# Neighbourhood mixer of a transformer trunk: queries two pairs ahead, keys projected apart, part of the output projection held back, values packed as high beside low parts

## Chip, cores and metric

One core of a Trainium2 chip runs the whole program. The metric is device time in microseconds (us) of one execution. PE is the matmul engine, PEld its weight load, DVE the vector engine, ACT the scalar engine, POOL GpSimd, SP the queue that issues most transfers.

## The reference

Four post-norm sublayers in each of two layers: half-step FFN, token mixer, memory attention, half-step FFN, on 512 tokens of width 1024 in float32. The mixer of layer 0 is called AB below. The change lies in the mixer of layer 1, C, for 16 heads of width 64 on an 8 x 64 grid:

```python
q, k, v = jnp.split(h @ w_in, 3, axis=-1)
...
    s = jnp.einsum('bwhd,bawjhd->bhwaj', q_r, k_nb).astype(jnp.float32) * scale
    s = s + bias.astype(jnp.float32)[None]
    p = jax.nn.softmax(s.reshape(B, C_HEADS, GRID_W, kh * kw), axis=-1)
...
    return jnp.einsum('bhwaj,bawjhd->bwhd', p, v_nb)
...
return o @ w_out
```

Each token sees all 8 rows and a window of 16 columns around its own. Then x = LN(alpha*x + mixer(x)).

## The kernel before

Float32 accuracy is reached with split operands: every operand is a high part and a low part (`split`: ACT writes the high part, DVE the difference), and a product is three matmuls (`mm3`: high x high, high x low, low x high).

`mixer_c` works in eight pairs of heads. For a pair, `queries_keys` projects queries and keys (24 matmuls of 512 columns each, two PSUM banks), `weights_of` makes eight score blocks (two matmuls of 192 or 256 columns each, into a bank of tag "a"), adds the bias and takes the minimum on DVE, the exponential on ACT, and normalises (192-column blocks on DVE, 256-column blocks on POOL). `turned` transposes the weights on PE into four banks of tag "t" (two for each head), each drained by one ACT cast and one DVE subtraction. `attend` multiplies by the values into one bank of tag "d". `values` projects the values of four heads (two pairs) at once, into slabs that POOL first clears (`padded`), since the stationary operand of one head has zeros in the other head's columns.

In the loop, step `pair` holds the projections of pair+1 (on odd steps with the values of the next two pairs ahead of them), `turned` of its own weights, the scores of pair+1, and its own `attend`. The output projection is done at step 4 (for the first four pairs), at step 7 (two pairs) and after the loop (the last two, with the layer norm of each 128-token tile, the transposes of the normed tile, and then the memory attention).

All instructions are recorded first and put into an order by `Graph.emit`, a list scheduler with estimated durations; on the chip each engine runs its own list in that order. Banks and slabs are handed out by tag: 27 slabs, two raw weight buffers, 14 `t2` buffers, three banks "a", two "d", three "t". A bank is given out again when the last reader of its former contents is done. Every recorded instruction has line L140 in the profile, so instructions are told apart by their tiles: `a`, `d`, `t` are the banks.

Of the kernel before, what the change touches and what calls it, by code (L numbers as in the profile page):

```python
# [12 lines left out]
F32 = mybir.dt.float32  # L13
F32R = mybir.dt.float32r
# [3 lines left out]
ALU = mybir.AluOpType  # L18
AX = mybir.AxisListType

P = 128
D = 1024
S = 512
NT = S // P
# [225 lines left out]
class Kernel:  # L250
# [94 lines left out]
            )  # L345
        return got

    def w_rows(self, w, r0):

        src = w[r0 : r0 + 256, :].rearrange("(b p) f -> p b f", p=P)  # L350
        return self.weights([(lambda r: r, src)], (2, D), [lambda r, i=i: r[:, i, :] for i in range(2)])

# [53 lines left out]
        nc.vector.scalar_tensor_tensor(out=x, in0=x, scalar=nmu, in1=g, op0=ALU.add, op1=ALU.mult)  # L406
        nc.vector.scalar_tensor_tensor(out=x, in0=x, scalar=r, in1=b, op0=ALU.mult, op1=ALU.add)

    def down_bank(self, acts, wts, t, h, coef):

        ps = self.ps("d")
        for i, (act, w) in enumerate(zip(acts, wts)):
            self.mm3(ps, [z[:, t * P : (t + 1) * P] for z in act], w, i == 0, i == len(acts) - 1)
        v = self.x[t][:, h * 512 : (h + 1) * 512]
        self.nc.vector.scalar_tensor_tensor(out=v, in0=ps, scalar=coef, in1=v, op0=ALU.mult, op1=ALU.add)
# [494 lines left out]
    def mixer_c(self, ln_i, last):  # L910
# [2 lines left out]

        ends = [self.slab(F32R, (P, KB, P)) for _ in range(2)]

        def values(grp):

            wv = self.w_cols_k(w_in, 2 * D + 256 * grp)
            vp = [self.padded() for _ in range(2)]
            if grp == 0:  # L920
                for dst, lo in ((slice(64, 128), 0), (slice(0, 64), 448)):
                    nc.scalar.copy(ends[0][:, :, dst], self.xh[:, :, lo : lo + 64])
                    nc.vector.tensor_copy(ends[1][:, :, dst], self.xl[:, :, lo : lo + 64])
            for t in range(NT):
                ps = self.ps("a")
                for k in range(KB):
                    mv = [z[:, k % 4, :] for z in wv[k // 4]]
                    x = self.xT(k, 64 + t * P, 64 + (t + 1) * P) if t < 3 else [z[:, k, :] for z in ends]
                    self.mm3(ps[:, :256], x, mv, k == 0, k == KB - 1)
                for b in range(2):  # L930
                    dst = []
                    for z in vp[b]:
                        v = z[:, t].rearrange("p v c -> p (v c)")
                        dst.append(bass.AP(v.tensor, v.offset, [list(v.ap[0]), [192, 2], [1, 64]]))
                    self.split(ps[:, b * P : (b + 1) * P].rearrange("p (v c) -> p v c", v=2), *dst)
            return vp

        def queries_keys(w, b, first):


            cuts = [(0, 128), (128, 256), (256, 512)] if first else [(0, 512)]
            ps = self.ps("a")
            for lo, hi in cuts:
                self.project(w[0][b], ps, lo, hi)
            qs = self.pair()
            for s, z in enumerate(qs):
# [5 lines left out]
            ps = self.ps("a")  # L952
            for lo, hi in [(0, 256), (256, 512)] if first else cuts:
                self.project(w[1][b], ps, lo, hi)
            ks = [self.pair() for _ in range(2)]
            for s, (h, l) in enumerate(ks):
# [5 lines left out]
            return list(zip(qs, ks))  # L962

        def biases(pair):

# [15 lines left out]
                got.append(dst)  # L981
            return got

        def weights_of(qk, bias):

            got = []
            for (q, k), table in zip(qk, bias):
# [38 lines left out]

        def attend(pts, vp):
            po = self.ps("d")
            ends_ = bass.AP(po[:].tensor, po[:].offset, [list(po[:].ap[0]), [384, 2], [1, P]])
            for s in range(2):  # L1030
                for j in range(4):
                    dst = po[:, j * P : j * P + 256] if j < 3 else ends_
                    mv = [z[:, (j % 2) * 256 : (j % 2) * 256 + 256] for z in pts[s][j // 2]]
                    if j == 3:
                        mv = [z.rearrange("p (c n) -> p c n", c=2) for z in mv]
                    self.mm3(
                        dst, [z[:, j, s, :] for z in vp], mv, s == 0 and j == 0, s == 1 and j == 3, skip_group_check=True
                    )
            return self.split_t2(po)

        def weights_qk(grp):
            return self.w_cols(w_in, 256 * grp), self.w_cols(w_in, D + 256 * grp)

        vp = values(0)
        wqk = weights_qk(0)
        qk = queries_keys(wqk, 0, True)
        acts, us = [], weights_of(qk, biases(0))
        for pair in range(8):

            now = vp[pair % 2]  # L1050
            if pair % 2 == 1 and pair < 7:
                vp = values(pair // 2 + 1)
                wqk = weights_qk(pair // 2 + 1)
            if pair < 7:
                qk = queries_keys(wqk, (pair + 1) % 2, False)
            if pair == 4:
                self.down(acts[:4], self.w_rows(w_out, 0) + self.w_rows(w_out, 256), 1.0 / ALPHA)
            if pair == 7:
                self.down(acts[4:6], self.w_rows(w_out, 512), 1.0 / ALPHA)
            pts = turned(us)  # L1060
            if pair < 7:
                us = weights_of(qk, biases(pair + 1))
            acts.append(attend(pts, now))
        gb = self.load_ln(ln_i)
        self.down(acts[6:], self.w_rows(w_out, 768), 1.0 / ALPHA, {"gb": gb, "last": last})


    def memory(self, i, ln_i, last):
# [195 lines left out]
```

## Time and profile before

| what | us |
|---|---|
| median of 3 runs (2286.45 to 2290.6) | 2288.22 |
| profiled execution | 2287.07 |
| its span | 2285.3 |

| engine | busy us | share of the span | instructions |
|---|---|---|---|
| PE | 2227.2 | 97% | 11376 |
| DVE | 1414.9 | 62% | 2124 |
| ACT | 873.2 | 38% | 1418 |
| POOL | 298.8 | 13% | 407 |

Busy is an average over stages. What a stage can give is what PE loses in it: idle time, and time at a lower granted clock. The mixer C and the tail that leads into the memory attention lie from about 1468.7 to 1757.4 us of the span.

### The profile page before, as it was taken

Reading aid. Unit: us, or ns where it says so; the run is one execution under the profiler, and the core shown is the slowest. Engines: PE = TensorE matmul, PEld = TensorE weight load, DVE = VectorE, ACT = ScalarE, POOL = GpSimd, SP = SyncE. Lnnn points to the kernel's source line nnn. Section 1 sums busy time; section 2 is a strip of 40 time slices with the busy share of each in tenths; the row PEclk is TensorE's granted clock in tenths of the full one; section 3 lists DMA queues with packets and bytes.
Section 4 is the critical chain, followed back from the end, with each engine's and each line's share of the span. In section 5 each row is a group of like instructions: output and inputs, shape, how many; then the busy total and the mean of one; then the engine's idle time right before and its main releaser. Section 6 shows DMA issues by size and latency. Waiting matters only on the chain.

```text
span 2285.3 us, 28345 instructions
## 1 busy us (share of the span) xinstructions
PE 2227.2 (97%) x11376; PEld 1887.8 (83%) x11376; DVE 1414.9 (62%) x2124; ACT 873.2 (38%) x1418; POOL 298.8 (13%) x407
## 2 busy tenths in 40 slices
PE   8999999999999999999999999989998999999998
PEld 7888888778898888888988888888787988888886
DVE  5666646788745666664666665556667557566653
ACT  4333323476433433333333333344454444333331
POOL 0000203543100100020100012223221001000021
PEclk9999999999999999999999999989999999999999
DMA  6333241003423233324233224121122433312241
GB/s 203 127 118 111 83 146 45 19 20 101 140 93 126 78 111 111 111 83 134 79 111 109 71 78 164 49 65 65 61 79 93 131 128 111 108 63 75 90 145 37
DMA packets 168211, 221.09 MB, mean 97 GB/s; under 512 B 6160, under 2 KB 136848, under 8 KB 168080
## 3 DMA queue, kind: packets, MB, share of 16 engines
q1 hardware_dynamic: 165008, 208.80, 28.1%
q0 software_dynamic: 3072, 10.49, 1.4%
q8 instruction: 89, 1.46, 0.3%
q14 instruction: 42, 0.34, 0.1%
HBM read 217.17 MB, written 4.19 MB: 97 GB/s over the span
## 4 chain that ended last, share of the span: by engine, by line
PE 92%; DVE 4%; ACT 1%; POOL 1%; DMA 1%; issue 1%; SPq 0%; POOLq 0%; ACTq 0%; DVEq 0%
PE a L140 58%; PE d L140 25%; PE t L140 9%; DVE slab L140 2%; DVE x L140 1%; POOL lny L140 1%; ACT junk L140 1%; ACT slab L140 1%; DVE t L140 1%; DMA x<-x 0%; DVE xl L140 0%; DMA raw<-mem_w_kv 0%; ACT t L140 0%; SPq L140 0%; ACT xh L140 0%
## 5 line engine op out<-in xcount | busy, mean ns | idle before, releaser
L140 PE MATMUL a<-xh,slab 128*128 128x512 f32 (+2 forms) x3184 | 962.4, 383 | 0.0
L140 PEld LDWEIGHTS a<-xh,slab 128*128 128x128 f32 x3184 | 592.2, 188 | 116.0 <-DVE mn L140 0.2
L140 PE MATMUL d<-slab,slab 128*128 128x512 f32 (+2 forms) x2592 | 609.8, 384 | 12.6 <-ACT slab L140 8.8
L140 PE MATMUL a<-xl,slab 128*128 128x512 f32 (+2 forms) x1592 | 609.3, 383 | 0.0
L140 PEld LDWEIGHTS d<-slab,slab 128*128 128x128 f32 x2592 | 469.9, 190 | 108.4 <-ACT slab L140 12.6
L140 DVE TENSOR_TENSOR slab<-raw,slab 128x1024 fp32r<-128x1024 f32 x316 | 393.4, 1261 | 75.4 <-ACT slab L140 54.8
L140 ACT CAST slab<-raw 128x1024 fp32r<-128x1024 f32 x316 | 320.4, 1050 | 307.2 <-DMA raw<-ffn_w_gate 141.6
L140 PEld LDWEIGHTS a<-xl,slab 128*128 128x128 f32 x1592 | 299.8, 188 | 57.4
L140 DVE TENSOR_TENSOR slab<-slab,slab 128x1024 fp32r<-128x1024 f32 (+2 forms) x208 | 241.5, 1185 | 19.4 <-ACT slab L140 18.4
L140 ACT CAST slab<-slab 128x1024 fp32r<-128x1024 f32 (+1 forms) x144 | 140.2, 1001 | 238.5 <-DVE slab L140 238.1
L140 DVE TENSOR_TENSOR slab<-a,t 128x512 f32<-128x512 f32 x56 | 38.7, 692 | 270.2 <-PE a L140 270.2
L140 PE MATMUL a<-slab,slab 128*128 128x256 f32 (+2 forms) x1312 | 193.9, 296 | 7.4 <-DVE slab L140 3.7
L140 ACT CAST slab<-t 128x512 fp32r<-128x512 f32 (+1 forms) x213 | 118.2, 580 | 209.5 <-DVE t L140 137.8
L140 DVE SCALAR_TENSOR_TENSOR x<-d,x 128x512 f32<-128x512 f32 x232 | 158.2, 686 | 61.0 <-PE d L140 60.1
L140 PEld LDWEIGHTS a<-slab,slab 128*128 128x128 f32 x1312 | 171.8, 194 | 20.2 <-DVE slab L140 6.7
L140 POOL TENSOR_TENSOR x<-x,slab 128x512 f32<-128x512 f32 x24 | 46.0, 1947 | 782.2 <-DVE x L140 782.2
L140 DVE TENSOR_TENSOR slab<-t,slab 128x512 fp32r<-128x512 f32 (+1 forms) x213 | 134.3, 655 | 20.1 <-ACT slab L140 19.1
L140 ACT ACTIVATE t<-a 128x512 f32<-128x512 f32 (+2 forms) x104 | 57.4, 552 | 227.9 <-PE a L140 205.8
L140 PE MATMUL t<-slab,slab 128*128 128x512 f32 x576 | 143.2, 391 | 0.0
L140 PE MATMUL a<-slab,xh 128*128 128x256 f32 (+1 forms) x576 | 125.4, 313 | 4.2 <-ACT xh L140 4.2
L140 PEld LDWEIGHTS t<-slab,slab 128*128 128x128 f32 x576 | 106.7, 188 | 25.3 <-DVE slab L140 2.4
L140 POOL TENSOR_TENSOR t<-t,l 128x256 f32<-128x256 f32 (+2 forms) x104 | 86.5, 847 | 303.4 <-DVE l L140 303.4
(84 smaller groups left out, 1643.9 us busy)
## 6 DMA issues: line engine op xcount, KB each, us to landing
raw<-ffn_w_gate SPq DMA_DIRECT2D x40, 1024.0 KB
raw<-ffn_w_up SPq DMA_DIRECT2D x40, 1024.0 KB
slab<-ffn_w_down SPq DMA_DIRECT2D x64, 512.0 KB
raw<-ffn_w_down SPq DMA_DIRECT2D x12, 1024.0 KB
raw<-mem_w_kv SPq DMA_DIRECT2D x8, 1024.0 KB
raw<-mem_w_kv SPq DMA_DIRECT2D x16, 512.0 KB
raw<-mem_w_q SPq DMA_DIRECT2D x8, 1024.0 KB
raw<-mem_w_o SPq DMA_DIRECT2D x8, 1024.0 KB
```

The lines of the kernel that those rows point to most:

```text
L140: op.call = lambda: fn(*args, **kw)
```

## The change

- The projections of one pair become two functions. `queries(pair)` uses a bank "d" and is recorded two pairs ahead, between `turned` and the scores; `keys(pair)` uses a bank "t" and stays one pair ahead, at the step's start.
- `values` is called for one 128-token tile at a time: two tiles behind each `attend`, in a bank "t". The slabs hold for each head 64 columns of high parts beside 64 of low parts; nothing is cleared.
- `attend` makes two matmuls a block in place of three: the stationary operand is [high | low], the moving one the weights' high, then low part, so a fourth product (low x low) is in it too. Each head has a bank "d" of its own; the high half (partitions 0 to 63) and the low half (64 to 127) are added by an ACT copy and a DVE addition per head, and the sum is split again by one ACT cast and one DVE subtraction.
- The output projection: the first four pairs' part becomes eight single banks ("a"), `share(0)` to `share(7)`: two after `turned` of step 6, one behind its `attend`, two ahead of `turned` of step 7, three behind it. Their weights come in four 512 KB loads. The last four pairs' part all stands after the loop, in the banks with the layer norm.

```diff
-        def values(grp):
-
-            wv = self.w_cols_k(w_in, 2 * D + 256 * grp)
-            vp = [self.padded() for _ in range(2)]
...
-                        dst.append(bass.AP(v.tensor, v.offset, [list(v.ap[0]), [192, 2], [1, 64]]))
-                    self.split(ps[:, b * P : (b + 1) * P].rearrange("p (v c) -> p v c", v=2), *dst)
-            return vp
...
+        def values(grp, t):
+
+            if t == 0:
+                wv[0] = self.w_cols_k(w_in, 2 * D + 256 * grp)
+                vp[grp] = [self.slab(F32R, (P, 2, 4, 2, 64)) for _ in range(2)]
...
+            ps = self.ps("t" if grp else "a")
+            for k in range(KB):
+                mv = [z[:, k % 4, :] for z in wv[0][k // 4]]
+                x = self.xT(k, 64 + t * P, 64 + (t + 1) * P) if t < 3 else [z[:, k, :] for z in ends]
+                self.mm3(ps[:, :256], x, mv, k == 0, k == KB - 1)
+            z = vp[grp][t // 2][:, t % 2]
+            self.split(ps[:, :256].rearrange("p (v c) -> p v c", v=4), z[:, :, 0], z[:, :, 1])
+
+        def queries(pair, first=False):
+
+            if pair % 2 == 0:
+                wq[0] = self.w_cols(w_in, 128 * pair)
+            ps = self.ps("a" if first else "d")
+            for lo, hi in [(0, 128), (128, 256), (256, 512)] if first else [(0, 512)]:
+                self.project(wq[0][pair % 2], ps, lo, hi)
+            qs[pair] = self.pair()
...
+        def keys(pair, first=False):
+
+            if pair % 2 == 0:
+                wk[0] = self.w_cols(w_in, D + 128 * pair)
+            ps = self.ps("a" if first else "t")
+            for lo, hi in [(0, 256), (256, 512)] if first else [(0, 512)]:
+                self.project(wk[0][pair % 2], ps, lo, hi)
+            ks[pair] = [self.pair() for _ in range(2)]
...
-        def attend(pts, vp):
-            po = self.ps("d")
...
+        def attend(pts, pair):
+            pos = [self.ps("d") for _ in range(2)]
+            for s, po in enumerate(pos):
...
+                    dst = po[:, j * P : j * P + 256] if j < 3 else po.rearrange("p (c n) -> p c n", c=4)[:, 0:4:3]
+                    v = vp[pair // 2][j // 2][:, j % 2, 2 * (pair % 2) + s].rearrange("p z c -> p (z c)")
+                    for i, z in enumerate(pts[s][j // 2]):
+                        mv = z[:, (j % 2) * 256 : (j % 2) * 256 + 256]
+                        mv = mv.rearrange("p (c n) -> p c n", c=2) if j == 3 else mv
+                        nc.tensor.matmul(
+                            dst, v, mv, start=j == 0 and i == 0, stop=j == 3 and i == 1, skip_group_check=True
+                        )
+
+            o = self.t2(F32)
+            for s, po in enumerate(pos):
+                y = o[64 * s : 64 * s + 64]
+                nc.scalar.copy(y, po[64:128])
+                nc.vector.tensor_tensor(out=y, in0=po[0:64], in1=y, op=ALU.add)
...
+        def share(n):
+
+            h, t = divmod(n, 4)
+            if t == 0:
+                wo[h] = [z for r in range(2) for z in self.w_rows(w_out, 256 * r, 512 * h)]
+            self.down_bank(acts[:4], wo[h], t, h, 1.0 / ALPHA, "a")
...
+        for t in range(NT):
+            values(0, t)
+        queries(0, True)
+        keys(0, True)
+        queries(1)
+        us = weights_of(0)
...
             if pair < 7:
-                qk = queries_keys(wqk, (pair + 1) % 2, False)
-            if pair == 4:
-                self.down(acts[:4], self.w_rows(w_out, 0) + self.w_rows(w_out, 256), 1.0 / ALPHA)
-            if pair == 7:
-                self.down(acts[4:6], self.w_rows(w_out, 512), 1.0 / ALPHA)
+                keys(pair + 1)
+            else:
+                for n in range(3, 5):
+                    share(n)
             pts = turned(us)
+            if pair < 6:
+                queries(pair + 2)
+            else:
+                for n in (0, 1) if pair == 6 else (5, 6, 7):
+                    share(n)
             if pair < 7:
-                us = weights_of(qk, biases(pair + 1))
-            acts.append(attend(pts, now))
+                us = weights_of(pair + 1)
+            acts.append(attend(pts, pair))
+            if pair < 6:
+                for t in range(2):
+                    values(pair // 2 + 1, 2 * (pair % 2) + t)
+            elif pair == 6:
+                share(2)
         gb = self.load_ln(ln_i)
-        self.down(acts[6:], self.w_rows(w_out, 768), 1.0 / ALPHA, {"gb": gb, "last": last})
+        self.down(acts[4:], self.w_rows(w_out, 512) + self.w_rows(w_out, 768), 1.0 / ALPHA, {"gb": gb, "last": last})
```

In the order of the instructions this shows at three places. In PE's list, at step 2 (keys of pair 3 and weights of pair 2; `a_2283` and `t_2283` are the bank of the keys before and now, `t_2286` to `t_2292` the four turned banks, `d_2299` the bank of the queries of pair 4), this stood before:

```order
L140 MATMUL a_2283_2364<-xh_2_83,slab_2239_2320 128x512
L140 MATMUL t_2286_2367<-ident_1_78,t2_2257_2338 128x128 x3
...
L140 MATMUL t_2288_2369<-ident_1_78,t2_2258_2339 128x128 x2
...
L140 MATMUL t_2290_2371<-ident_1_78,t2_2268_2349 128x128 x3
...
L140 MATMUL a_2301_2382<-slab_2284_2365,slab_2282_2363 128x192
...
L140 MATMUL d_2320_2401<-slab_2287_2368,slab_2222_2303 128x256
...
L140 MATMUL t_2292_2373<-ident_1_78,t2_2269_2350 128x128 x2
...
L140 MATMUL d_2320_2401<-slab_2287_2368,slab_2222_2303 128x256
```

And this stands now:

```order
L140 MATMUL t_2283_2364<-xh_2_83,slab_2237_2318 128x512
L140 MATMUL t_2286_2367<-ident_1_78,t2_2255_2336 128x128 x3
...
L140 MATMUL t_2288_2369<-ident_1_78,t2_2256_2337 128x128 x2
...
L140 MATMUL d_2299_2380<-xh_2_83,slab_2295_2376 128x512
...
L140 MATMUL t_2290_2371<-ident_1_78,t2_2266_2347 128x128 x3
...
L140 MATMUL t_2292_2373<-ident_1_78,t2_2267_2348 128x128 x2
...
L140 MATMUL d_2299_2380<-xh_2_83,slab_2296_2377 128x512
...
L140 MATMUL a_2308_2389<-slab_2284_2365,slab_2250_2331 128x192 x2
...
L140 MATMUL d_2327_2408<-slab_2287_2368,slab_2229_2310 128x256 x3
```

Before, three turned banks, two half-done score blocks and one value product stand between the last projection and the fourth bank. Now 14 of the 24 query matmuls stand between the second and the third bank, and the other ten between the fourth and the scores.

In DVE's list at the same place (draining the keys' bank and the turned banks), before:

```order
L140 TENSOR_TENSOR slab_2284_2365<-a_2283_2364,slab_2284_2365 64x512 x2
L140 TENSOR_TENSOR slab_2287_2368<-t_2286_2367,slab_2287_2368 128x512
L140 TENSOR_TENSOR slab_2289_2370<-t_2288_2369,slab_2289_2370 128x512
L140 TENSOR_TENSOR slab_2285_2366<-a_2283_2364,slab_2285_2366 64x512 x2
L140 TENSOR_TENSOR slab_2291_2372<-t_2290_2371,slab_2291_2372 128x512
L140 ISA t2_2298_2379,mn_2302_2383<-a_2301_2382,t2_2296_2377 128x192
```

And now, where the keys' bank has tag "t" too, so that `t_2290` waits for its last reader (slab_2285):

```order
L140 TENSOR_TENSOR slab_2284_2365<-t_2283_2364,slab_2284_2365 64x512 x2
L140 TENSOR_TENSOR slab_2287_2368<-t_2286_2367,slab_2287_2368 128x512
L140 TENSOR_TENSOR slab_2289_2370<-t_2288_2369,slab_2289_2370 128x512
L140 TENSOR_TENSOR slab_2285_2366<-t_2283_2364,slab_2285_2366 64x512 x2
L140 TENSOR_TENSOR slab_2291_2372<-t_2290_2371,slab_2291_2372 128x512
L140 TENSOR_TENSOR slab_2293_2374<-t_2292_2373,slab_2293_2374 128x512
L140 TENSOR_TENSOR slab_2342_2423<-raw_2340_2421,slab_2341_2422 128x1024
L140 ISA t2_2305_2386,mn_2309_2390<-a_2308_2389,t2_2303_2384 128x192
...
L140 SCALAR_TENSOR_TENSOR slab_2300_2381<-d_2299_2380,slab_2300_2381 64x512 x2
```

The draining has the same order as before; behind it, a weight split and the first two score blocks now stand ahead of the draining of the queries' bank `d_2299`.

In PE's list in the tail (`d_2597` and up before, `d_2599` and up now: banks of the last output products; x0 to x3: the normed tiles, transposed into `t`), before:

```order
L140 MATMUL d_2597_2678<-slab_2576_2657,slab_2549_2630 128x512
...
L140 MATMUL d_2598_2679<-slab_2576_2657,slab_2549_2630 128x512
...
L140 MATMUL t_2586_2667<-ident_1_78,x0_4_85 128x128 x4
...
L140 MATMUL d_2605_2686<-slab_2576_2657,slab_2549_2630 128x512
...
L140 MATMUL d_2606_2687<-slab_2576_2657,slab_2549_2630 128x512
...
L140 MATMUL t_2594_2675<-ident_1_78,x1_5_86 128x128 x4
...
L140 MATMUL t_2602_2683<-ident_1_78,x2_6_87 128x128 x4
```

And now:

```order
L140 MATMUL d_2599_2680<-slab_2573_2654,slab_2437_2518 128x512
...
L140 MATMUL t_2588_2669<-ident_1_78,x0_4_85 128x128 x4
...
L140 MATMUL d_2600_2681<-slab_2573_2654,slab_2437_2518 128x512
...
L140 MATMUL d_2607_2688<-slab_2573_2654,slab_2437_2518 128x512
...
L140 MATMUL t_2596_2677<-ident_1_78,x1_5_86 128x128 x4
...
L140 MATMUL d_2608_2689<-slab_2573_2654,slab_2437_2518 128x512
...
L140 MATMUL t_2604_2685<-ident_1_78,x2_6_87 128x128 x4
...
L140 MATMUL t_2615_2696<-ident_1_78,raw_2614_2695 128x128 x4
```

Six matmuls a bank (two pairs) have become twelve (four pairs), and the transposes of a tile stand among the products of the tile after next.

## Rows read from the trace of the kernel before

**Rows 1.** The page, part 1 (busy us, share, instructions) and the granted clock by slice

```profile
PE 2227.2 (97%) x11376; PEld 1887.8 (83%) x11376; DVE 1414.9 (62%) x2124; ACT 873.2 (38%) x1418; POOL 298.8 (13%) x407
...
PEclk9999999999999999999999999989999999999999
```

**Rows 2.** Windows over mixer C and its tail: window, length, busy by engine, clock

```profile
1468.70:1498.20 29.50, 28.16 (x233) 27.39 (x232) 15.38 (x26) 9.01 (x20) 5.47 (x6) 1.00 0.24 74
1498.20:1530.50 32.30, 26.29 (x122) 21.83 (x120) 19.51 (x50) 18.44 (x43) 8.27 (x18) 0.79 0.22 72
...
1563.50:1584.50 21.00, 19.30 (x102) 16.59 (x100) 17.09 (x33) 13.50 (x29) 11.78 (x19) 0.92 0.20 63
...
1728.00:1757.40 29.40, 21.31 (x103) 16.70 (x102) 24.83 (x42) 13.14 (x22) 7.26 (x8) 0.88 0.10 32
sum 288.70, PE 263.38 PEld 229.67 DVE 183.91 ACT 131.26 POOL 78.25; mean PE 29.26 PEld 25.52 DVE 20.43 ACT 14.58 POOL 8.69
```

**Rows 3.** Windows over the six stretches of half clock in that stage

```profile
1500.90:1511.10 10.20, 7.96 (x23) 6.35 (x24) 8.09 (x26) 6.99 (x20) 4.74 (x9) 0.50 0.10 32
...
sum 27.20, PE 23.80 PEld 21.84 DVE 22.46 ACT 17.00 POOL 6.59; mean PE 3.97 PEld 3.64 DVE 3.74 ACT 2.83 POOL 1.10
```

**Rows 4.** Timeline at step 0: start, us, engine, what, in brackets idle before

```profile
1520.23 1.17 ACT L140 CAST slab<-a 64x512 fp32r<-64x512 f32 x2 [3.18 <-PE a L140]
...
1523.39 0.39 PE L140 MATMUL d<-slab,slab 128*128 128x256 f32 x1 [1.44 <-ACT slab L140]
...
1523.47 1.29 DVE L140 TENSOR_TENSOR slab<-t,slab 128x512 fp32r<-128x512 f32 x2
...
1524.22 0.66 PE L140 MATMUL t<-ident,t 128*128 128x128 f32 x4 [0.22 <-DVE slab L140]
...
1524.80 1.40 DVE L140 TENSOR_TENSOR slab<-a,slab 64x512 fp32r<-64x512 f32 x2
```

**Rows 5.** Waits from 1498 to 1757: total us, times, longest

```profile
PE d L140 <- ACT slab L140: 7.5, 6, 1.4
PE t L140 <- DVE nmu L140: 4.2, 1, 4.2
```

**Rows 6.** Groups by form, 1478 to 1728: busy us, mean ns, idle before

```profile
L140 DVE TENSOR_TENSOR slab<-raw,slab 128x1024 fp32r<-128x1024 f32 x26 | 34.9, 1361 | 0.1
...
L140 ACT CAST slab<-raw 128x1024 fp32r<-128x1024 f32 x25 | 25.5, 1050 | 0.1
...
L140 DVE TENSOR_TENSOR slab<-a,slab 64x512 fp32r<-64x512 f32 x32 | 22.0, 689 | 32.0 <-PE t L140 21.0 <-ACT slab L140 10.6
L140 DVE TENSOR_TENSOR slab<-t,slab 128x512 fp32r<-128x512 f32 x32 | 21.2, 687 | 0.6 <-ACT slab L140 0.2
...
L140 POOL MEMSET slab<- 128x1024 f32 x10 | 9.3, 954 | 29.5 <-PE d L140 23.3 <-PE a L140 6.2
```

**Rows 7.** The chain in order of time: start, us, what

```profile
559.31 5.91 DMA raw<-mem_w_kv
...
1618.11 11.03 PE a L140 x48
...
1757.37 22.65 PE a L140 x189
```

**Rows 8.** Windows over mixer AB and its tail, columns as in group 2

```profile
240.00:480.00 240.00, 239.35 (x1111) 195.28 (x1110) 155.87 (x279) 91.79 (x165) 72.60 (x81) 1.00 0.22 70
...
555.00:600.00 45.00, 40.69 (x224) 33.45 (x223) 34.55 (x54) 19.18 (x31) 5.28 (x8) 1.00 0.32 101
```

**Rows 9.** Timeline in the tail of mixer C

```profile
1745.80 1.27 DVE L140 SCALAR_TENSOR_TENSOR x<-x,lny,slab 128x1024 f32<-128x1024 f32 x1
...
1747.22 1.94 PE L140 MATMUL t<-ident,x 128*128 128x128 f32 x8 [4.17 <-DVE nmu L140]
```

**Rows 10.** Timeline: normalising on DVE beside POOL, and without

```profile
1531.38 1.23 DVE L140 TENSOR_SCALAR t<-t,l 128x192 f32<-128x192 f32 x2
...
1660.82 0.55 DVE L140 TENSOR_SCALAR t<-t,l 128x192 f32<-128x192 f32 x2
```

More of the change, by code (lines that the diff above doesn't have):

```diff
@@ L346, in w_cols512, with w_rows @@
         return got
-    def w_rows(self, w, r0):
+    def w_rows(self, w, r0, c0=None):
+        if c0 is not None:
+            src = w[r0 : r0 + 256, c0 : c0 + 512].rearrange("(b p) f -> p b f", p=P)
+            hi, lo = self.weights([(lambda r: r, src)], (2, 512), [lambda r: r])[0]
+            return [(hi[:, b], lo[:, b]) for b in range(2)]
         src = w[r0 : r0 + 256, :].rearrange("(b p) f -> p b f", p=P)
@@ L407, in layer_norm, with down_bank @@
         nc.vector.scalar_tensor_tensor(out=x, in0=x, scalar=r, in1=b, op0=ALU.mult, op1=ALU.add)
-    def down_bank(self, acts, wts, t, h, coef):
-        ps = self.ps("d")
+    def down_bank(self, acts, wts, t, h, coef, tag="d"):
+        ps = self.ps(tag)
         for i, (act, w) in enumerate(zip(acts, wts)):
@@ L914, in mixer_c @@
         ends = [self.slab(F32R, (P, KB, P)) for _ in range(2)]
-        def values(grp):
-            wv = self.w_cols_k(w_in, 2 * D + 256 * grp)
-            vp = [self.padded() for _ in range(2)]
[L920 to L933, printed above, removed]
-                        dst.append(bass.AP(v.tensor, v.offset, [list(v.ap[0]), [192, 2], [1, 64]]))
-                    self.split(ps[:, b * P : (b + 1) * P].rearrange("p (v c) -> p v c", v=2), *dst)
-            return vp
@@ L938, in queries_keys @@
[L938 to L946, printed above, removed]
+        def values(grp, t):
+            if t == 0:
+                wv[0] = self.w_cols_k(w_in, 2 * D + 256 * grp)
+                vp[grp] = [self.slab(F32R, (P, 2, 4, 2, 64)) for _ in range(2)]
+                if grp == 0:
+                    for dst, lo in ((slice(64, 128), 0), (slice(0, 64), 448)):
+                        nc.scalar.copy(ends[0][:, :, dst], self.xh[:, :, lo : lo + 64])
+                        nc.vector.tensor_copy(ends[1][:, :, dst], self.xl[:, :, lo : lo + 64])
+            ps = self.ps("t" if grp else "a")
[5 more added lines that the diff above has]
+            self.split(ps[:, :256].rearrange("p (v c) -> p v c", v=4), z[:, :, 0], z[:, :, 1])
@@ L947, in queries_keys @@
+        def queries(pair, first=False):
[5 more added lines that the diff above has]
+            qs[pair] = self.pair()
+            for s, z in enumerate(qs[pair]):
                 own, other = slice(64 * s, 64 * s + 64), slice(64 - 64 * s, 128 - 64 * s)
@@ L951, in queries_keys @@
                 )
[L952 to L956, printed above, removed]
+        def keys(pair, first=False):
[5 more added lines that the diff above has]
+            ks[pair] = [self.pair() for _ in range(2)]
+            for s, (h, l) in enumerate(ks[pair]):
                 own, other = slice(64 * s, 64 * s + 64), slice(64 - 64 * s, 128 - 64 * s)
@@ L961, in queries_keys @@
                     nc.vector.tensor_tensor(out=l[half], in0=ps[own], in1=h[own].bitcast(F32), op=ALU.subtract)
-            return list(zip(qs, ks))
         def biases(pair):
@@ L982, in biases, with weights_of @@
             return got
-        def weights_of(qk, bias):
+        def weights_of(pair):
             got = []
-            for (q, k), table in zip(qk, bias):
+            for q, k, table in zip(qs.pop(pair), ks.pop(pair), biases(pair)):
                 both = [self.t2(F32), self.t2(F32)]
@@ L1025, in turned @@
             return pts
-        def attend(pts, vp):
-            po = self.ps("d")
-            ends_ = bass.AP(po[:].tensor, po[:].offset, [list(po[:].ap[0]), [384, 2], [1, P]])
-            for s in range(2):
+        def attend(pts, pair):
+            pos = [self.ps("d") for _ in range(2)]
+            for s, po in enumerate(pos):
                 for j in range(4):
[L1032 to L1047, printed above, removed]
+                    dst = po[:, j * P : j * P + 256] if j < 3 else po.rearrange("p (c n) -> p c n", c=4)[:, 0:4:3]
[6 more added lines that the diff above has]
+                        )
@@ new lines, in attend @@
+            o = self.t2(F32)
[3 more added lines that the diff above has]
+                nc.vector.tensor_tensor(out=y, in0=po[0:64], in1=y, op=ALU.add)
+            return self.split_pair(o)
+        def share(n):
[3 more added lines that the diff above has]
+            self.down_bank(acts[:4], wo[h], t, h, 1.0 / ALPHA, "a")
@@ L1048, in mixer_c @@
+        vp, qs, ks, acts = {}, {}, {}, []
+        wv, wq, wk, wo = [None], [None], [None], {}
+        for t in range(NT):
[4 more added lines that the diff above has]
+        us = weights_of(0)
         for pair in range(8):
[L1050 to L1053, printed above, removed]
             if pair < 7:
-                qk = queries_keys(wqk, (pair + 1) % 2, False)
```

## The prediction

> **What bounds the kernel now.** I read the page's busy table and clock line first: PE is busy for 97% of the span at nearly full clock, and no other engine comes near it [rows 1]. So the kernel is bound by PE, and a change can win only by taking matmuls out or by filling the places where PE idles or runs at half clock. The clock line shows one dull slice; windows over it show that this is mixer C, the stage that the change rewrites. In the 288.7 us from 1468.7 to 1757.4, PE is busy for 263.4, so it idles for 25.3, and of these 8.1 lie in the tail and 6.0 in the first steps [rows 2]. The granted clock in the stage is below 1 in four windows. Cut into its six low stretches, it stands at 0.50 (1.2 in place of 2.4 GHz) for 27.2 us, in which PE is busy for 23.8; work done at half rate takes twice its time, so this costs 23.8 / 2 = 11.9 us [rows 3]. Together the stage loses 25.3 + 11.9 = 37.2 us.
>
> Where does PE idle? The timeline of step 0 shows the pattern that repeats in most steps: PE has done its transposes and stands for 1.44 us until ACT has cast the first turned bank (which comes behind two of the key copies), and again 0.22 us for the fourth bank [rows 4]. The table of waits counts six such waits, 7.5 us, and one wait of 4.2 us in the tail on the layer norm's chain [rows 5]. Before the stretches of half clock PE had stood in such waits; in the first one it still idles for 2.2 of 10.2 us [rows 3]. No wait of PE or ACT on a weight transfer is in that table.
>
> **The change part by part.**
>
> *Products.* Value products go from 24 to 16 a pair, 64 fewer in all. 189 matmuls of 256 columns in a row took 22.65 us, 0.12 each [rows 7]: 64 x 0.12 = 7.7 us of PE are gone, and they lie on the path, since PE is the bound. All other matmuls stay; the output products are 192 as before, only moved.
>
> *Filler behind the transposes.* 24 query matmuls (512 columns, 11.03 / 48 = 0.23 each [rows 7], 5.5 us) now stand between the turned banks and the first value product. The wait of 1.44 us and its companions are covered by them, and at the start by `queries(1)` and `keys(1)` the waits on the first keys and scores. If all of it is covered and nothing new waits, only what lies outside the steps stays.
>
> *New waits on banks.* The keys' bank now has tag "t", so the third turned bank must wait until it is drained. Count from the end of the keys' projection. ACT works on three key copies, two turned banks and the fourth copy at 1.17 / 2 = 0.58 each; DVE takes two key differences (1.40), then two turned ones (1.29), then two key ones (1.40) [rows 4]. DVE can start at 0.7, is at the turned banks at about 2.5 (ACT is there no earlier) and done with them at 3.9, and frees the bank at about 5.2. PE has eight transposes (about 1.1; four took 0.66 with the last one's drain [rows 4]) and 14 query matmuls (3.2) until then, and asks at 4.3: it stands for about 0.9 to 1.0 us, of which a busy table shows 0.8, since the matmul in flight still drains. Queued behind it on PE are the fourth bank, ten query matmuls and the scores, and so the exponentials of the next pair. Behind that, eight score blocks share three "a" banks, and the second head's value products need the queries' bank, behind a weight split (1.36 us on DVE [rows 6]) in every second step. I take 0.5 a step for these, between 0 (all hidden) and 1.4 (the split's whole length). That is 1.3 us for each of seven steps, 9.1 in all. Where DVE is late at the keys, each 0.7 us of lateness comes on top.
>
> *Engines beside PE.* An attend gains two DVE additions of 64x512 in place of a difference of 512, and one more difference: 2 x 0.69 more for each pair, 11 us. Eight output additions (16 banks in place of 24 outside the tail's own) go, 8 x 0.69 = 5.5 us [rows 6], and the value splits become half as many. DVE is busy for 183.9 of 288.7 us [rows 2]; 189 of 262 would be 72%. It is covered by PE's work on the average, and dear only where it comes in bursts. POOL loses 16 clears of 0.95 us, 15 us [rows 6]; ten lie in these rows. They are worth nothing by themselves, for POOL is busy for 78 of 289 us [rows 2]. SP issues two more loads (four of half the size in place of two), hidden behind the keys and scores of step 6; exposed, they cost what the last rival says. The bias loads and bias work on POOL stay where they were.
>
> One row speaks against more DVE work here. Normalising two 192-column blocks took 1.23 us beside a POOL instruction and 0.55 us without one [rows 10]. The Trainium skill (SBUF — State Buffer, Who interferes with whom) says that DVE instructions with two SBUF inputs, or in a two-port mode, share an exclusive port pair with GpSimd, and that the second to come is fully blocked. The trace agrees for the normalising with the numbers above; for the new difference (both inputs in SBUF) no row of this stage shows it. By the rule it could be held up as the normalising was, an estimate of (1.23 - 0.55) / 2 = 0.34 us a pair on DVE; by its row alone it costs 0.69 and no more.
>
> *Tail.* Before, PE does six matmuls a bank (2.8 us a tile) while DVE needs two additions (1.4), two passes of the norm (2 x 1.27 [rows 9]) and the split of the transposes (as long as two turned banks, 1.29 [rows 4]), some 5.2 us a tile. So PE waits, once for 4.17 us [rows 9], and the clock falls (0.88 [rows 2]); idle is 8.1 us. With twelve a bank PE has 5.5 us a tile and the norm hides beside it. Mixer AB's tail has just this form (twelve a bank, then the memory attention), and idles for 4.3 of 45 us at full clock [rows 8]. I take 4.3.
>
> *Sum.* Left after the change: 1.3 us in the first window (the lead-in, unchanged), 1.0 at the first scores, 9.1 in steps 0 to 6, 0.5 in step 7, 4.3 in the tail, 1.5 for one stretch of half clock, since waits of about 1 us remain: 17.7. Gain: 7.7 + 37.2 - 17.7 = 27.2 us. The profiled execution took 2287.07 (span 2285.3), which makes 2259.9; it lies 1.15 under the median of the runs, so I predict **2261 us**.
>
> Bounds: mixer AB's main part, built in the same way, idles for 0.65 in 240 us [rows 8], and steps that lose only 0.4 each (3.2) leave 9.3 in all with 0.5 at the start and no half clock: gain 35.6, time 2252.6. At the other end a step loses as much as the worst between 1563.5 and 1584.5: 1.7 idle and 21 x 0.08 = 1.7 of clock [rows 2], 3.4 for each of seven steps: 23.8 + 1.3 + 1.0 + 0.5 + 4.3 = 30.9, gain 14.0, time 2274.
>
> **Rivals.**
>
> - *Full cover* (2253): the bank waits hide, because DVE reaches the keys early. For it speaks mixer AB; against it the count above, in which 5.2 stands against 4.3.
> - *DVE late in every step* (2274): the weight splits, the longer attend and the shared port push the keys' draining back, PE waits as long as before and its clock falls again. For it speaks that DVE is already busy for 17.1 of 21.0 us in a step without values [rows 2]; against it that each step now has 48 of the 96 value matmuls of two pairs in it, 5.8 us of PE time.
> - *The cover is worth nothing* (2280.5): every wait returns in another place, and only the 7.7 us of products are won.
> - *Slower* (2294): weights come late. Queries two pairs ahead, keys and values now ask for their loads one by one through two raw buffers. A load that PE must wait for costs a transfer of about 5.9 us (the chain's row for 1 MB, its own wait) [rows 7], a cast of 1.05 and a difference of 1.36 [rows 6], 8.3 us. There are nine such loads after the first three; from the fourth that is exposed (33.2 us against 27.2) the kernel is slower, at 2288.2 + 6. Against it: nothing waited for one before, and the number of bytes is the same over a stage a tenth shorter.
>
> **How the numbers follow.** Forecast 0.58, full cover 0.16, DVE late 0.15, cover worth nothing 0.04, weights late 0.03, no change to be seen for a reason that I don't know 0.04. About 0.2% (4.6 us) is what a measurement of this kernel can tell from no change. The first four are faster, 0.93, of which I move 0.01 to slower for what the cases leave out: faster 0.92, same 0.04, slower 0.04. The range takes in full cover and DVE late with the runs' spread of some 2 to 4 us: 2249 to 2276.
>
> **What the profile after would show.** Right: 11312 matmuls; in mixer C no wait of PE on an ACT cast of over 1 us behind the transposes; new waits of the third turned bank on DVE, 0.5 to 1.2 us, about seven times; PE idle of about 16 us in the stage, half of it in the steps; at most two stretches of half clock; a tail idle of 4 to 5 us. Wrong: PE waits of over 2 us in each step, several stretches at 1.2 GHz, or a wait of ACT on c_w_in or c_w_out, each of which would put the time at 2270 or more; or no waits at "t" at all, which would put it near 2253.

## The result and the profile after

The changed kernel takes 2249.53 us (median of four runs, 2248.52 to 2250.93), the kernel before 2287.34: 37.8 us less, a ratio of 0.9833 with an interval from 0.9816 to 0.985. I had predicted 2261. The profiled execution has a span of 2248.3 us against 2285.3.

The page of the changed kernel, part 1 (beside [rows 1]) and its clock line:

```profile
PE 2207.0 (98%) x11312; PEld 1871.7 (83%) x11312; DVE 1420.1 (63%) x2116; ACT 882.7 (39%) x1418; POOL 287.0 (13%) x391
...
PEclk9999999999999999999999999999999999999999
```

There are 64 matmuls fewer, and the dull slice is gone. Mixer C and its tail, which took the stretch from 1468.7 to 1757.4, now end at about 1722; that is 35.4 of the 37.0 us. The two windows do not hold quite the same work: the one before has 1553 matmuls and this one 1497, which is 56 fewer and not 64, since eight of the memory attention's, about 1.0 us of PE, now stand ahead of its end. The same windows, cut anew, stand beside [rows 2]; the row after them is the only stretch of half clock that is left in the stage, beside [rows 3]:

```profile
1468.70:1498.20 29.50, 29.00 (x239) 28.27 (x238) 15.21 (x22) 9.81 (x17) 1.83 (x2) 1.00 0.23 72
1498.20:1522.50 24.30, 23.32 (x130) 19.61 (x129) 19.52 (x49) 18.89 (x42) 7.08 (x16) 1.00 0.18 55
1522.50:1535.00 12.50, 12.32 (x82) 11.11 (x81) 8.19 (x20) 5.34 (x17) 6.83 (x11) 1.00 0.33 107
1535.00:1690.00 155.00, 151.92 (x913) 131.64 (x912) 123.22 (x257) 95.76 (x211) 45.46 (x80) 1.00 0.25 82
1690.00:1721.96 31.96, 27.74 (x141) 23.42 (x140) 24.77 (x40) 12.70 (x21) 7.78 (x8) 0.89 0.20 66
sum 253.26, PE 244.31 PEld 214.05 DVE 190.92 ACT 142.51 POOL 68.98; mean PE 48.86 PEld 42.81 DVE 38.18 ACT 28.50 POOL 13.80
...
1713.40:1720.20 6.80, 5.60 (x25) 5.21 (x26) 3.98 (x6) 1.17 (x2) 1.77 (x2) 0.50 0.46 154
```

The first two figures of each row are the window's length and PE's busy time in it. PE idles for 253.26 - 244.31 = 8.95 us, and half clock costs 5.60 / 2 = 2.8: 11.75 in all, against 37.2 before and 17.7 in my sum. Of the idle, 4.2 lie in the tail, as forecast, but only 4.24 from 1498.2 to 1690, where I had put 10.6. The clock is full in every step. The table of waits for the stage (total us, times, longest) beside [rows 5] has no wait on a cast behind the transposes any more:

```profile
PE a L140 <- ACT slab L140: 2.1, 2, 1.9
PE t L140 <- DVE x L140: 1.4, 2, 0.9
PE t L140 <- DVE slab L140: 1.3, 3, 0.6
PE a L140 <- DVE slab L140: 1.2, 1, 1.2
...
PE d L140 <- DVE slab L140: 0.9, 4, 0.3
```

The two waits on bank "a" (1.9 and 1.2) are in the tail. The third line is where my forecast had seven waits of 0.8 us: there are three, 1.3 us together, and only one of them (0.45, in step 0) is at a third turned bank; the others are at step 5's first bank (0.26) and at a keys' projection (0.58). The timeline at step 2 shows why. PE's transposes into the first two turned banks start at 1557.47, DVE works on key and turned differences in one run from 1560.25 to 1565.01, and PE starts on the third turned bank at 1561.71:

```profile
1557.47 1.03 PE L140 MATMUL t<-ident,t 128*128 128x128 f32 x8
...
1558.92 0.68 DVE L140 TENSOR_TENSOR slab<-t,slab 64x512 fp32r<-64x512 f32 x1 [0.68 <-ACT slab L140]
...
1560.25 4.76 DVE L140 TENSOR_TENSOR slab<-t,slab 64x512 fp32r<-64x512 f32 x7 [0.65 <-ACT slab L140]
...
1560.85 0.62 PE L140 MATMUL d<-xh,slab 128*128 128x512 f32 x2
...
1561.30 0.39 PE L140 MATMUL d<-xl,slab 128*128 128x512 f32 x1
1561.71 0.42 PEld L140 LDWEIGHTS t<-ident,t 128*128 128x128 f32 x4 [0.45 <-DVE slab L140]
1561.71 1.25 PE L140 MATMUL t<-ident,t 128*128 128x128 f32 x8
```

By the order of the instructions the last key difference is the fifth of DVE's seven (two of turned banks come second and third, two of the keys after them, 0.69 each), so the keys' bank is free at about 1563.7, two microseconds after PE has begun to write the third turned bank. PE cannot have waited for it. The difference of the first turned bank, the second of the seven, ends at about 1561.6, and there PE begins: the weight load's 0.45 is a wait for that bank. PE's own row shows no idle time, since the matmul before it counts as busy until it has drained. In the built program the banks of this step are:

```
keys t_2283 bank 0 | turned t_2286 bank 2, t_2288 bank 1, t_2290 bank 2, t_2292 bank 1
```

The third turned bank takes the bank of the first one, and the fourth that of the second; the same holds in steps 0 to 6. The remark ahead of the prediction that `t_2290` waits for the keys' last reader is wrong too.

### The profile page after: what moved, and what is told of

It is laid out like the page before. It is cut to its first block, busy times and chain, and to the rows that moved or that the text cites. A ratio compares the mean times of both kernels' runs of the same rounds, so it can differ in the third digit from the quotient of the medians.

```text
span 2248.3 us, 28157 instructions
## 1 busy us (share of the span) xinstructions
PE 2207.0 (98%) x11312; PEld 1871.7 (83%) x11312; DVE 1420.1 (63%) x2116; ACT 882.7 (39%) x1418; POOL 287.0 (13%) x391
## 5 line engine op out<-in xcount | busy, mean ns | idle before, releaser
L140 PE MATMUL a<-xh,slab 128*128 128x512 f32 (+1 forms) x2960 | 890.8, 382 | 0.0
L140 PEld LDWEIGHTS a<-xh,slab 128*128 128x128 f32 x2960 | 549.1, 188 | 107.1
L140 PE MATMUL d<-slab,slab 128*128 128x512 f32 (+2 forms) x2432 | 572.5, 384 | 4.7 <-DVE slab L140 2.8
L140 PE MATMUL a<-xl,slab 128*128 128x512 f32 (+1 forms) x1480 | 565.0, 382 | 0.0
L140 PEld LDWEIGHTS d<-slab,slab 128*128 128x128 f32 x2432 | 441.1, 188 | 94.3 <-DVE slab L140 4.2
L140 ACT CAST slab<-t 128x512 fp32r<-128x512 f32 (+3 forms) x261 | 143.5, 572 | 225.9 <-DVE t L140 142.0
L140 PE MATMUL a<-slab,slab 128*128 128x256 f32 (+3 forms) x1336 | 204.9, 303 | 6.2 <-DVE slab L140 2.6
L140 DVE TENSOR_TENSOR slab<-t,slab 128x512 fp32r<-128x512 f32 (+3 forms) x261 | 164.3, 654 | 42.7 <-ACT slab L140 41.5
L140 PE MATMUL t<-slab,slab 128*128 128x512 f32 (+1 forms) x648 | 152.1, 379 | 0.0
L140 PE MATMUL a<-slab,xh 128*128 128x256 f32 (+1 forms) x432 | 98.1, 319 | 4.1 <-ACT xh L140 4.0
```

Of the source, the lines that this page charges most:

```text
L140: op.call = lambda: fn(*args, **kw)
```

## The experiments

Each interval of a ratio is about 0.0015 to either side, 3.4 us, so that two kernels must lie some 3 us apart to be told apart by their times alone. Differences are given to the changed kernel's 2249.5.

**A third product.** One more product in each block of `attend`:

```diff
-                    for i, z in enumerate(pts[s][j // 2]):
+                    for i, z in enumerate(pts[s][j // 2] + pts[s][j // 2][:1]):
...
-                            dst, v, mv, start=j == 0 and i == 0, stop=j == 3 and i == 1, skip_group_check=True
+                            dst, v, mv, start=j == 0 and i == 0, stop=j == 3 and i == 2, skip_group_check=True
```

> The changed kernel with a third product in each block of values times weights: the high beside low values times the high weights once more, 64 matmuls of 256 columns in all (so the attention of mixer C adds that product twice). All else is as in the changed kernel. Theory (PE is the bound, and a product costs its 0.12 us of issue): 64 x 0.12 = 7.7 us more, about 2257. Rival 1 (the removed products were worth more than I put down, since PE's busy time in the stage fell by 10 us after the half clock is taken out): 64 x 0.16 = 10 us, about 2260. Rival 2 (a product is partly cover for waits of the attend): 4 us or less, 2253.5 or below.

It took 2261.11 (ratio 0.9885, 0.987 to 0.9899), 11.6 more. By the number alone this is the first rival, but the trace says otherwise. Its longest wait from 1650 to 1680 (total us, times, longest):

```profile
PE t L140 <- DVE slab L140: 3.3, 1, 3.3
```

And its window right behind it, columns as in group 2:

```profile
1663.50:1670.30 6.80, 5.73 (x18) 4.86 (x19) 5.99 (x9) 3.38 (x6) 0.00 (x0) 0.50 0.00 0
```

One new wait of 3.3 us, at step 6's third turned bank, and a stretch of half clock behind it (5.73 / 2 = 2.9) are more than what goes beyond 7.7, 3.9 us; the tail's stretch of half clock is shorter in return (3.4 us in place of 6.8). What made DVE late there stands on ACT:

```profile
1659.63 1.05 ACT L140 CAST slab<-raw 128x1024 fp32r<-128x1024 f32 x1 [7.05 <-DMA raw<-c_w_out]
1660.59 1.16 ACT L140 CAST slab<-t 64x512 fp32r<-64x512 f32 x2
```

ACT stands for 7.05 us until a load of the output weights has landed, and the key copies come behind that cast in its list; DVE's differences wait for the copies, and PE for the bank. So the excess is one exposed weight load, the rival *slower* in a single place, and not a higher price of the products.

**Padded values.** The values, `attend` and its single bank as before, in the changed order:

```diff
-                vp[grp] = [self.slab(F32R, (P, 2, 4, 2, 64)) for _ in range(2)]
+                vp[grp] = [self.padded() for _ in range(2)]
...
-            return self.split_pair(o)
+                    v = [z[:, j, s, :] for z in vp[pair // 2][pair % 2]]
+                    self.mm3(dst, v, mv, s == 0 and j == 0, s == 1 and j == 3, skip_group_check=True)
+            return self.split_t2(po)
```

> The changed kernel with the values as before: padded tiles cleared on POOL, three products, one bank for both heads and one difference, and no additions on DVE. Theory (only PE's matmuls count; POOL's clears and DVE's eleven us are covered): 7.7 us more, 2256 to 2258.5. Rival 1 (DVE's additions were on the path): the loss is 4 us or less, 2253.5 or below. Rival 2 (the clears or the four slabs more that values then hold delay the loads): over 11 us, 2260 or above.

2257.03 (0.9867, 0.9852 to 0.9882): 7.5 more, as the theory has it. The packed values are worth about their 64 matmuls, 7.7 us; an effect of POOL's clears or DVE's additions of under some 3 us either way would not show beside that.

**Queries one pair ahead.**

```diff
-        queries(1)
...
             if pair < 7:
+                queries(pair + 1)
                 keys(pair + 1)
...
-            if pair < 6:
-                queries(pair + 2)
```

> The changed kernel with the queries one pair ahead, at the head of the step before the keys, so that nothing of them stands behind the turned banks. Theory (the queries cover the waits behind the transposes): six waits of 1.0 to 1.4 us return, 6 to 8 us, with 2 to 8 us of half clock: 2257 to 2266, and PE again waits over 1 us on ACT's casts of turned banks. Rival (the scores and the value matmuls, which the changed kernel also spreads over the steps, cover these waits as well): 3 us or less, 2252.5 or below.

2267.07 (0.9911, 0.9894 to 0.9927): 17.5 more, the largest of all, just above what I expected. The waits of PE from 1498 to 1710:

```profile
PE d L140 <- ACT slab L140: 9.6, 6, 2.9
PE a L140 <- ACT slab L140: 3.3, 6, 1.2
```

The sum of the windows over its four stretches of half clock in the steps (at 1517.7, 1568.9, 1596.2 and 1647.4):

```profile
sum 13.60, PE 13.42 PEld 13.19 DVE 13.19 ACT 8.65 POOL 0.61; mean PE 3.36 PEld 3.30 DVE 3.30 ACT 2.16 POOL 0.15
```

The six waits on ACT's casts are back (7.5 us before the change [rows 5]), one of 2.9 in step 0 and five of 1.3, and half clock costs 13.42 / 2 = 6.7 in the steps. Scores and values between the steps' parts do not cover them; the queries do. The edit also takes the queries of pair 1 from the start; how much of the 17.5 that is by itself was not measured.

**The output share as before.**

```diff
-                for n in range(3, 5):
-                    share(n)
+            if pair == 4:
+                self.down(acts[:4], self.w_rows(w_out, 0) + self.w_rows(w_out, 256), 1.0 / ALPHA)
+            if pair == 7:
+                self.down(acts[4:6], self.w_rows(w_out, 512), 1.0 / ALPHA)
...
-        self.down(acts[4:], self.w_rows(w_out, 512) + self.w_rows(w_out, 768), 1.0 / ALPHA, {"gb": gb, "last": last})
+        self.down(acts[6:], self.w_rows(w_out, 768), 1.0 / ALPHA, {"gb": gb, "last": last})
```

> The changed kernel with the output projection placed as before: four pairs' share in step 4, the next two pairs' in step 7, two pairs in the tail. Theory (twelve matmuls a bank hide the norm in the tail, and the held share covers the transposes of steps 6 and 7): the tail idles 8 us in place of 4.2 and its clock falls, 4 to 7 us more, and step 6 loses about 1.4: 2254 to 2259. Rival (the tail's waits hide behind the memory attention's first work anyway): 2 us or less, 2251.5 or below.

2259.05 (0.9875, 0.9861 to 0.989): 9.5 more, at the upper end of the theory. The wait on the norm in the tail returns:

```profile
PE t L140 <- DVE nmu L140: 3.7, 1, 3.7
```

With it returns a stretch of half clock, by window:

```profile
1715.20:1728.90 13.70, 8.62 (x40) 7.48 (x38) 11.70 (x18) 6.50 (x12) 3.67 (x4) 0.50 0.11 35
```

PE idles for 5.1 us of that one stretch and loses 8.62 / 2 = 4.3 more to the clock.

**Making the third turned bank wait.** Two small readings on DVE (0.16 us each, where I had put 0.08) keep the first two turned banks until the keys are drained; in the built program the third turned bank then does take the keys' bank (`t_2287` and `t_2296`, both bank 2).

```diff
+                if n == 0 and kl:
+                    for ps in pss:
+                        nc.vector.tensor_tensor(
+                            out=self.small(1, "hold", 1), in0=ps[:, 511:512], in1=kl[1][1][:, 511:512].bitcast(F32), op=ALU.add
+                        )
```

> The changed kernel with the wait that my forecast assumed: in steps 0 to 6 two readings of one column on DVE (0.08 us each), which also read the last key difference, keep the first two turned banks until the keys' bank is drained, so that the third turned bank can have no bank before that. Theory (the price in the forecast was right, but in the changed kernel the third turned bank takes the bank of the first one, which is long free): seven waits of 0.8 to 1.0 us, 5.6 to 7 us, with 0 to 3 us of half clock: 2255 to 2259.5. Rival (the price was wrong too: DVE reaches the keys early, or other ready matmuls are put there): 2 us or less, 2251.5 or below.

2250.51 (0.9837, 0.9824 to 0.9851): 1.0 more, not to be told from nothing. Here my theory fell. The timeline at step 2 of this kernel, PE and DVE:

```profile
1558.23 1.03 PE L140 MATMUL t<-ident,t 128*128 128x128 f32 x8
...
1563.65 0.61 PE L140 MATMUL d<-xh,slab 128*128 128x512 f32 x2
1564.58 1.06 PE L140 MATMUL t<-ident,t 128*128 128x128 f32 x8 [0.31 <-DVE slab L140]
...
1564.46 0.35 DVE L140 TENSOR_TENSOR hold<-t,slab 128x1 f32<-128x1 f32 x2
```

And of its waits from 1530 to 1690 the one that was meant to cost:

```profile
PE t L140 <- DVE slab L140: 1.9, 6, 0.5
```

The wait is there, but small: five of the six stand at the third turned bank, 0.26 to 0.32 each, and the longest, 0.5, at a keys' projection (step 0, ahead of this window, has one of 0.74). The instructions were put in another order: 22 of the 24 query matmuls now stand ahead of the third turned bank in place of 14, so that PE comes to it 6.35 us after the first transposes, where it came after 4.24 in the changed kernel. The order is made from what is free when, and the filler has moved to where the hole would have been. My price held the order of the changed kernel fixed.

**More work on DVE.** The last difference of each `attend` repeated, four times or twice:

```diff
-            return self.split_pair(o)
+            hi, lo = self.split_pair(o)
+            for _ in range(4):
+                nc.vector.tensor_tensor(out=lo, in0=o, in1=hi.bitcast(F32), op=ALU.subtract)
+            return hi, lo
```

> The changed kernel with the last difference of each attend written four times more on DVE: 4 x 8 x 0.69 = 22 us of DVE, 84% of the stage in place of 75%. Theory (DVE's work beside PE is covered): 3 us or less, 2249 to 2252.5. Rival (DVE is late in every step): 2.8 us a pair come on the path in most steps, 10 us or more, 2260 or above.

> As more_vector_work, with two repeated differences a pair in place of four: 2 x 8 x 0.69 = 11 us more on DVE, about as much as the new attend adds. With four, 22 us of DVE brought 10.6 us of time. Theory (DVE has some slack in each step, and beyond it all comes on the path): the first half brings less than half of it, 0 to 4 us, 2249 to 2253.5. Rival (DVE's lateness is proportional, so that the changed kernel already pays for its own additions): 5 us or more, 2254.5 or above.

Four repeats: 2260.09 (0.9879, 0.9866 to 0.9893), 10.6 more; the rival's side. Two repeats: 2251.71 (0.9848, 0.9835 to 0.9862), 2.2 more; the theory's side. With four, PE's timeline at step 2 reads:

```profile
1563.78 1.25 PE L140 MATMUL t<-ident,t 128*128 128x128 f32 x8 [1.74 <-DVE slab L140]
```

And the waits of the stage:

```profile
PE t L140 <- DVE slab L140: 4.8, 4, 1.7
PE d L140 <- DVE slab L140: 3.6, 5, 2.3
```

By the medians the first 11 us of DVE cost 2.2 (within the interval) and the next 11 cost 8.4. The wait is the one at the third turned bank, now for the first turned bank to be drained. It is long in two steps only (1.74 at step 2 and 1.54 at step 4; one of 1.04 is at step 5's first bank), so DVE is not late in every step. One part is the experiment's own: the wait of 2.3 is in the tail, where the last pair's low part is read only after its last rewriting.

**Keys in the scores' banks.** `ps = self.ps("a")` in `keys` for every pair.

> The changed kernel with the keys in the banks of the scores (tag a) in place of those of the turned blocks (tag t). Theory (which banks the keys have matters little, since the turned banks reuse their own): within 2 us, 2247.5 to 2251.5. Rival (that the keys have banks apart from the scores is worth a wait in each step): the first scores of a step wait for the keys' bank, 0.5 us or more in seven steps, 2253 or above.

2249.91 (0.9834, 0.9821 to 0.9847): 0.4 more. Which banks the keys have is worth nothing that can be measured here.

**The memory's start ahead of the tail.** What is left in the tail are the two waits on bank "a". The timeline there, in the changed kernel:

```profile
1711.57 1.16 ACT L140 ACTIVATE junk<-x,nmu 128x1024 bf16<-128x1024 f32 x1
...
1712.71 0.58 ACT L140 CAST slab<-t 128x512 fp32r<-128x512 f32 x1
...
1713.35 0.95 PE L140 MATMUL a<-slab,slab 128*128 128x256 f32 x3 [1.90 <-ACT slab L140]
...
1713.57 1.28 DVE L140 SCALAR_TENSOR_TENSOR x<-x,nmu,slab 128x1024 f32<-128x1024 f32 x1
...
1714.76 0.68 DVE L140 TENSOR_TENSOR slab<-t,slab 128x512 fp32r<-128x512 f32 x1
...
1715.50 2.29 PE L140 MATMUL a<-slab,slab 128*128 128x256 f32 x9 [1.20 <-DVE slab L140]
```

The next stage's memory is transposed only here, and its cast stands behind the norm's squares on ACT, its difference behind a pass of the norm on DVE. Its input does not depend on the tail, so it can be had earlier; `turn_memory` is the first loop of `memory`, taken out:

```diff
+        ws = self.w_rows(w_out, 512) + self.w_rows(w_out, 768)
+        self.mem_turned = self.turn_memory()
         gb = self.load_ln(ln_i)
-        self.down(acts[4:], self.w_rows(w_out, 512) + self.w_rows(w_out, 768), 1.0 / ALPHA, {"gb": gb, "last": last})
+        self.down(acts[4:], ws, 1.0 / ALPHA, {"gb": gb, "last": last})
...
+        mt = self.mem_turned or self.turn_memory()
```

> The changed kernel with the loading, transposing and splitting of the memory for the second memory stage put ahead of the tail's projection (they do not depend on the tail). Theory (the two waits of 1.9 and 1.2 us at the tail's end, on the cast and the difference of the first memory bank, and the half clock behind them, 2.8 us, are what the tail still loses): 3 to 6 us less, 2243.5 to 2246.5. Rival (the wait only moves: to the memory's keys' weights, or to the last tile's norm): within 1.5 us, 2248 to 2251.

> As memory_start_early, with the memory's load, transposes and splits put ahead of the tail in mixer AB too. Theory (mixer AB's tail loses at the same place, some 2 us idle and 1.5 us of half clock): 2 to 4 us less than memory_start_early, 2239.5 to 2242. Rival (there the memory's first weights are late, or the two loads through the two raw buffers get in the way): 2243 or above.

In mixer C alone: 2243.71 (0.9808, 0.9794 to 0.9821), 5.8 less. In mixer AB too: 2237.35 (0.9784, 0.9771 to 0.9798), 12.2 less than the changed kernel and 49.5 less than the kernel before beside it; below what I expected, since mixer AB's tail gave 6.4 by the medians and not 2 to 4. In the profiled executions mixer C with its tail is 7.7 and 8.0 us shorter than in the changed kernel, and AB's tail 5.5; ahead of AB's tail, which the edits leave alone, both ran some 3 us longer, with a stretch of half clock at 491 us. So 1 to 3 us between two executions can come from a part that no edit touched. The tail of mixer C in the last one, by window (columns as in group 2):

```profile
1690.00:1716.00 26.00, 25.69 (x158) 22.54 (x157) 23.64 (x37) 13.76 (x23) 5.08 (x8) 1.00 0.36 120
```

PE idles for 0.3 of 26 us at full clock. This version beats both kernels.

## Why the prediction came out as it did

The kind and the place were right, the size was not: a gain of 27.2 us was forecast and 37.0 came, between the profiled spans. The time lies inside my range of 2249 to 2276 by half a microsecond, and nearer to the rival *full cover* (2253, chance 0.16) than to the forecast; that it fell inside is luck. The difference of about 10 us goes by steps.

- *What bounds the kernel* held. All but 1.6 us of the gain lies in the windows of mixer C and its tail (all but about 0.6 when the eight matmuls of the memory attention are set apart), and it came from matmuls removed and holes filled.
- *Products*, 7.7: borne out by the padded values, 7.5. The stage's PE time at full clock fell by (263.4 - 11.9) - (244.3 - 2.8) = 10.0 us, while the windows hold 56 matmuls fewer, 6.7. The 3.3 left over are waits that a busy table hides: two matmuls in a row take 0.62 us and one alone 0.39, so one that is followed adds 0.23, and 0.16 of a wait behind a matmul counts as busy. Counted from start to start in the two traces, outside half clock, PE starts late by 18.5 us less than before, and the table shows 15.2 of these as idle.
- *Filler behind the transposes*: right, and the largest part. Without it, and without the queries at the start, 17.5 us come back, two and a third times the products.
- *New waits on banks* is the step that failed. "The third turned bank must wait until it is drained" is wrong in the changed kernel: it takes the first turned bank's bank. The term was 1.3 for each of seven steps, 9.1, with 1.0 and 0.5 at the ends; measured from 1498.2 to 1690 are 4.24 in place of these 10.6. The 0.5 in it for what queues behind came as waits of 0.2 to 0.3 in four steps, at value products that need the queries' bank. Even where the wait was forced, the price was not 1.0 but about 0.3, since the queries moved into it. The reason that I gave for full cover ("DVE reaches the keys early") was not it either: DVE drains the keys 6.2 us after their projection's end, later than my 5.2, for its first key difference starts at 1558.92, 1.45 us after PE's first transposes where I had put 0.7, and it then waits 0.65 for ACT.
- *Lead-in*: 1.3 left unchanged in the sum, 0.5 measured.
- *Tail*: 4.3 forecast from mixer AB, 4.2 measured. The share's part as a whole is 9.5, with the clock.
- *Half clock*: one stretch for 1.5 forecast, 2.8 measured, in the tail; none in the steps, where the waits that I thought would bring it did not come.
- *Engines beside PE*: POOL's clears show no worth by the padded values, within some 3 us. DVE's share of the stage is 190.9 / 253.3 = 75% (72% forecast), and its cover is thinner than that share tells: 11 us of DVE work more in the stage cost 2.2, and 22 cost 10.6, with long waits in two of the steps and in the tail. *DVE late in every step* came in no run.
- The sum by these: 5.95 from the losses that did not come (17.7 - 11.75), 3.3 of hidden waits, about 0.6 outside the stage: 9.85 of the 9.8 by which 37.0 exceeds 27.2. It closes because the windows cover the whole gain; it is a split of it and no proof of the causes.
- *Slower, by late weights*: no wait of PE or ACT on c_w_in or c_w_out is in the table of the stage. The cover is not wide, though: with a third product one load of c_w_out was late (7.05 us on ACT, 3.3 on PE).

The three parts undone one by one cost 7.5, 17.5 and 9.5, and the keys' banks 0.4: 34.9 of the 37.8 us, so they nearly add up.

## What to carry to other kernels

A tag with three buffers tells which banks an instruction may have, not which it gets; before a wait on a bank is priced, look up in the built program whose bank it is, and ask whether the order would be made anew around the wait. Independent matmuls that can stand behind a transpose can be worth more than the matmuls that a cleverer product saves, here 17.5 against 7.5 us: the holes that came back cost their length and, behind four of six, half clock. Where the next stage begins with work that does not depend on the tail, put it ahead of the tail: that gave 12.2 us here for moving one loop ahead in two places.

## What the runs showed of the hardware

The new difference of `attend`, with both inputs in SBUF, is slower beside POOL. In the changed kernel's timeline it runs with one further difference in each of these groups; the first has no POOL instruction beside its difference, the second has the four of the last row:

```profile
1551.48 1.01 DVE L140 TENSOR_TENSOR slab<-t,slab 128x512 fp32r<-128x512 f32 x2
...
1597.78 1.46 DVE L140 TENSOR_TENSOR slab<-t,slab 128x512 fp32r<-128x512 f32 x2
...
1597.70 4.62 POOL L140 TENSOR_TENSOR t<-near,t 128x256 f32<-128x256 f32 x4
```

It costs 0.45 us more there, where my estimate from the normalising was 0.34. Taken by itself, the new difference takes 1.10 to 1.12 us in four of the eight pairs, each time beside POOL, and 0.68 to 0.69 in the other four. Differences that read a bank show nothing of the kind: a run of seven took 4.76 us at 1513.72, beside two POOL additions, and 4.76 at step 2, where POOL had none. The slower new difference agrees with the rule of the Trainium skill (SBUF — State Buffer, Who interferes with whom) that a DVE instruction with two SBUF inputs contends with a GpSimd instruction that reads SBUF.

Of the clock: in the kernel with four repeats on DVE, waits of up to 1.7 us in the steps left it at 1.00 from 1530 to 1690; with the queries one pair ahead, four stretches at 0.51 (3.4 us each) stood behind waits on ACT of 2.9, 1.3, 1.3 and 1.3 us, while behind two more of 1.3 us it stayed at 1.00. So the length of a wait alone does not tell whether the clock falls; what else does, no run here shows.
